# A rotary-embedding kernel: four neighbouring rows per partition, a cut first tile, and tables on another queue

## The chip, the cores and the metric

The kernel runs on one core of one Trainium2 chip. The metric is the device time of one execution in microseconds, as the median of several runs. The profile's span of the same execution is 1.8 to 2.1 us shorter than that time, mostly 1.8.

## The reference

```python
batch, seq, dim = 16, 512, 1024            # fp32, 33.5 MB in and 33.5 MB out
x = x.reshape(batch, seq, 16, 64)
x1, x2 = x[..., :32], x[..., 32:]
cos, sin = cos[None, :, None, :], sin[None, :, None, :]      # each (512, 32)
out = concatenate([x1 * cos - x2 * sin, x1 * sin + x2 * cos], axis=-1)
```

There is very little arithmetic for each byte. Every byte of x must come in once and every byte of the output must go out once.

## The kernel before

A tile is 128 sequence rows of four batches, 2 MB. Each partition holds one sequence row of each of the four batches, so what it holds lies in DRAM in four pieces of 4 KB, 2 MB apart. SyncE issues the loads. ScalarE converts a tile to bf16 and issues the stores. VectorE does two multiplies by tables that are stretched over heads, and then a subtraction and an addition that write fp32. There are three input buffers, two bf16 buffers and three output buffers. The last two tiles are cut into two and four pieces, and each piece takes a buffer of its own.

```python
if len(tiles) >= 2:
    t_last = tiles.pop()
    t_prev = tiles.pop()
    tiles += _split(t_prev, 2) + _split(t_last, 4)
...
NX = 3; NC = 2; NO = 3; NTMP = 2
...
cos_v = cos.rearrange("(sc p) j -> p sc j", p=P)              # pieces of 128 B
def x_tile_ap(t):
    sc, b0, nb = tiles[t]
    return x[b0:b0 + nb, sc * P:sc * P + P, :].rearrange("b s d -> s b d")   # pieces of 4 KB
...
# SyncE
for t in range(NT):
    if t >= NX:
        sp.wait_ge(sem_ci, t - NX + 1)          # the buffer's last tile has been converted
    sp.dma_start(x_sb[:, xb, 0:nb, :], x_tile_ap(t)).then_inc(sem_in[xb], 16)
    if t == 0:
        sp.dma_start(cos_sb[:], cos_v).then_inc(sem_tab, 16)
        sp.dma_start(sin_sb[:], sin_v).then_inc(sem_tab, 16)
...
# VectorE
ve.tensor_tensor(t1, xb_rows(cb, nb), coscat_b(sc, nb), mult)
ve.tensor_tensor(t2, xb_rows(cb, nb), sincat_b(sc, nb), mult).then_inc(sem_vp, 1)
if t >= NO:
    ve.wait_ge(sem_out[ob], 16 * (t // NO))     # the buffer's last store has landed
ve.tensor_tensor(orows[:, :, 0:HALF], t1[:, :, 0:HALF], t2[:, :, HALF:HD], subtract)
ve.tensor_tensor(orows[:, :, HALF:HD], t2[:, :, 0:HALF], t1[:, :, HALF:HD], add).then_inc(sem_vf, 1)
```

Of the kernel before, what the change touches and what calls it, by code (L numbers as in the profile page):

```python
# [7 lines left out]
def bass_split_heads_rope_kernel(  # L8
    nc: bass.Bass,
    x: bass.AP,  # L10
    cos: bass.AP,
    sin: bass.AP,
    num_heads: bass.AP,
    out: bass.AP,
):
    batch, seq, dim = x.shape
    H = int(num_heads)
    HD = dim // H
    HALF = HD // 2
    P = 128  # L20
    assert seq % P == 0
    NSC = seq // P

    NB = 4 if batch % 4 == 0 else batch
    tiles = []
    for sc in range(NSC):
        for b0 in range(0, batch, NB):
            tiles.append((sc, b0, NB))

    def _split(tile, parts):  # L30
        sc, b0, nb = tile
        if nb % parts != 0:
            return [tile]
        q = nb // parts
        return [(sc, b0 + i * q, q) for i in range(parts)]

    if len(tiles) >= 2:
        t_last = tiles.pop()
        t_prev = tiles.pop()
        tiles += _split(t_prev, 2) + _split(t_last, 4)  # L40
    NT = len(tiles)
    NBH = NB * H

    NX = 3
    NC = 2
    NO = 3
    NTMP = 2

    fp32 = mybir.dt.float32
    bf16 = mybir.dt.bfloat16  # L50
    mult = mybir.AluOpType.mult
    add = mybir.AluOpType.add
    subtract = mybir.AluOpType.subtract
    ACT_COPY = mybir.ActivationFunctionType.Copy

    with ExitStack() as stack:  # L56
        cos_sb = stack.enter_context(nc.sbuf_tensor([P, NSC, HALF], fp32))
        sin_sb = stack.enter_context(nc.sbuf_tensor([P, NSC, HALF], fp32))
        coscat_sb = stack.enter_context(nc.sbuf_tensor([P, NSC, HD], bf16))
        sincat_sb = stack.enter_context(nc.sbuf_tensor([P, NSC, HD], bf16))  # L60
        x_sb = stack.enter_context(nc.sbuf_tensor([P, NX, NB, dim], fp32))
        xb_sb = stack.enter_context(nc.sbuf_tensor([P, NC, NB, dim], bf16))
        o_sb = stack.enter_context(nc.sbuf_tensor([P, NO, NB, dim], fp32))
        tmp1_sb = stack.enter_context(nc.sbuf_tensor([P, NTMP, NBH, HD], bf16))
        tmp2_sb = stack.enter_context(nc.sbuf_tensor([P, NTMP, NBH, HD], bf16))
        sem_tab = stack.enter_context(nc.semaphore("sem_tab"))
        sem_tab2 = stack.enter_context(nc.semaphore("sem_tab2"))
        sem_in = [stack.enter_context(nc.semaphore(f"sem_in{i}")) for i in range(NX)]
        sem_out = [stack.enter_context(nc.semaphore(f"sem_out{i}")) for i in range(NO)]
        sem_ci = stack.enter_context(nc.semaphore("sem_ci"))  # L70
        sem_vp = stack.enter_context(nc.semaphore("sem_vp"))
        sem_vf = stack.enter_context(nc.semaphore("sem_vf"))
        block = stack.enter_context(nc.Block(no_gpsimd_drain=False))

        cos_v = cos.rearrange("(sc p) j -> p sc j", p=P)
        sin_v = sin.rearrange("(sc p) j -> p sc j", p=P)

        def x_tile_ap(t):
            sc, b0, nb = tiles[t]
            s0 = sc * P  # L80
            return x[b0:b0 + nb, s0:s0 + P, :].rearrange("b s d -> s b d")

        def out_tile_ap(t):
            sc, b0, nb = tiles[t]
            s0 = sc * P
            return out[b0:b0 + nb, s0:s0 + P, :, :].rearrange("b s h d -> s b (h d)")

        def xb_rows(cb, nb):
            return xb_sb[:, cb, 0:nb, :].rearrange("p b (h d) -> p (b h) d", h=H)

        def o_rows(ob, nb):
            return o_sb[:, ob, 0:nb, :].rearrange("p b (h d) -> p (b h) d", h=H)

        def coscat_b(sc, nb):
            return coscat_sb[:, sc, None, :].broadcast_to([P, nb * H, HD])

        def sincat_b(sc, nb):
            return sincat_sb[:, sc, None, :].broadcast_to([P, nb * H, HD])

        def uses(nbuf, b):  # L100
            return (NT - b + nbuf - 1) // nbuf

        @block.sync
        def _(sp):
            for t in range(NT):
                xb = t % NX
                _, _, nb = tiles[t]
                if t >= NX:
                    sp.wait_ge(sem_ci, t - NX + 1)
                sp.dma_start(x_sb[:, xb, 0:nb, :], x_tile_ap(t)).then_inc(sem_in[xb], 16)  # L110
                if t == 0:
                    sp.dma_start(cos_sb[:], cos_v).then_inc(sem_tab, 16)  # L112
                    sp.dma_start(sin_sb[:], sin_v).then_inc(sem_tab, 16)

        @block.scalar
        def _(ae):
            ae.wait_ge(sem_tab, 32)
            last = None
            for sc in range(NSC):
                last = ae.activation(coscat_sb[:, sc, 0:HALF], cos_sb[:, sc, :], ACT_COPY)  # L120
                last = ae.activation(coscat_sb[:, sc, HALF:HD], cos_sb[:, sc, :], ACT_COPY)  # L121
                last = ae.activation(sincat_sb[:, sc, 0:HALF], sin_sb[:, sc, :], ACT_COPY)  # L122
                last = ae.activation(sincat_sb[:, sc, HALF:HD], sin_sb[:, sc, :], ACT_COPY)  # L123
            assert last is not None
            last.then_inc(sem_tab2, 1)

            LEAD = 2
            for it in range(NT + LEAD):
                t = it
                if t < NT:  # L130
                    xb = t % NX
                    cb = t % NC
                    _, _, nb = tiles[t]
                    ae.wait_ge(sem_in[xb], 16 * (t // NX + 1))
                    if t >= NC:
                        ae.wait_ge(sem_vp, t - NC + 1)
                    ae.activation(  # L137
                        xb_sb[:, cb, 0:nb, :], x_sb[:, xb, 0:nb, :], ACT_COPY
                    ).then_inc(sem_ci, 1)
                u = it - LEAD  # L140
                if u >= 0:
                    ob = u % NO
                    _, _, nbu = tiles[u]
                    ae.wait_ge(sem_vf, u + 1)
                    ae.dma_start(out_tile_ap(u), o_sb[:, ob, 0:nbu, :]).then_inc(sem_out[ob], 16)
            for b in range(NO):
                ae.wait_ge(sem_out[b], 16 * uses(NO, b))

        @block.vector
        def _(ve):  # L150
            for t in range(NT):
                sc, _, nb = tiles[t]
                cb = t % NC
                tb = t % NTMP
                ob = t % NO
                nbh = nb * H
                if t == 0:
                    ve.wait_ge(sem_tab2, 1)
                ve.wait_ge(sem_ci, t + 1)
                if t >= NTMP:  # L160
                    ve.wait_ge(sem_vf, t - NTMP + 1)
                t1 = tmp1_sb[:, tb, 0:nbh, :]
                t2 = tmp2_sb[:, tb, 0:nbh, :]
                ve.tensor_tensor(t1, xb_rows(cb, nb), coscat_b(sc, nb), mult)  # L164
                ve.tensor_tensor(  # L165
                    t2, xb_rows(cb, nb), sincat_b(sc, nb), mult
                ).then_inc(sem_vp, 1)
                ve.wait_ge(sem_vp, t + 1)
                if t >= NO:
                    ve.wait_ge(sem_out[ob], 16 * (t // NO))  # L170
                orows = o_rows(ob, nb)
                ve.tensor_tensor(  # L172
                    orows[:, :, 0:HALF], t1[:, :, 0:HALF], t2[:, :, HALF:HD], subtract
                )
                ve.tensor_tensor(  # L175
                    orows[:, :, HALF:HD], t2[:, :, 0:HALF], t1[:, :, HALF:HD], add
                ).then_inc(sem_vf, 1)


# [31 lines left out]
```

## Time and profile before

| | before |
|---|---|
| time, median of 16 runs | 167.83 us |
| span of the profiled run (its own time: 168.56 us) | 166.7 us |
| bytes moved | 67.26 MB |
| DMA rate from 30 to 155 us | 421 GB/s |
| VectorE busy | 143.9 us |
| VectorE's first and last instruction | 14.37 and 163.6 us |

The profiled run was the slowest of these 16. The other runs of this kernel whose spans are listed have 165.9 to 166.3 us.

The page of the kernel before, in part: the row of DMA busy tenths over 40 equal slices of the span, the rate in each slice, and the packet count.

```profile
DMA  5999999999999999999999999999999999999974
GB/s 187 368 399 419 410 412 388 423 424 422 423 420 421 424 422 423 419 422 423 423 422 420 421 423 424 421 419 420 422 425 420 420 421 423 424 419 421 421 302 190
DMA packets 18082, 67.26 MB, mean 403 GB/s; under 512 B 1696, under 2 KB 1696, under 8 KB 18080
```

The DMA engines are busy from the first slice to the last. The packet count is the number of descriptors, and their sizes are those of the contiguous pieces: 16,384 records of 4 KB carry data and 1,024 of 128 B carry the tables. Nearly all of the rest, 672, have 4 B, which is 16 for each of the 42 DMAs; I take them for the semaphore updates.

The stretch table of the kernel before. A row gives a stretch of time, its length, the busy time of VectorE (DVE), ScalarE (ACT) and GpSimd (POOL) with their instruction counts, TensorE's clock, the DMA share and GB/s.

```profile
2.00:14.00 12.00, 0.00 (x0) 5.28 (x18) 0.00 (x0) 1.00 1.02 379
14.00:30.00 16.00, 15.56 (x7) 9.60 (x4) 0.00 (x0) 1.00 1.02 408
30.00:120.00 90.00, 88.75 (x41) 34.06 (x10) 0.00 (x0) 1.00 1.02 421
120.00:155.00 35.00, 31.12 (x21) 10.61 (x6) 0.00 (x0) 1.00 1.03 421
155.00:160.20 5.20, 5.13 (x9) 1.06 (x1) 0.00 (x0) 1.00 1.03 421
160.20:166.70 6.50, 3.37 (x6) 0.00 (x0) 0.00 (x0) 1.00 0.49 199
```

There are two losses around a steady 421 GB/s: a slow start, and 6.5 us at the end at 199 GB/s. In the middle both the DMA and VectorE are nearly full, so busy shares alone do not say which of them is the bound.

The timeline of the kernel before at three places: the tables arrive (8.74), VectorE starts (14.37), and in the tail the store of the last full tile is issued (141.87), VectorE waits (154.71) and finishes. Columns are start, duration, engine, line, operation, shapes, and the idle time before it with what ended it.

```profile
8.74 0.23 ACT L120 ACTIVATE coscat_sb<-cos_sb 128x32 bf16<-128x32 f32 x1 [6.72 <-DMA sin_sb<-in_sin_dram]
...
14.37 2.29 DVE L164 TENSOR_TENSOR tmp_sb<-xb_sb,coscat_sb 128x4096 bf16<-128x4096 bf16 x1 [14.37 <-ACT xb_sb L137]
...
141.87 0.38 ACTq L145 DMA_DIRECT2D out_dram<-o_sb  x1
...
154.71 0.69 DVE L172 TENSOR_TENSOR o_sb<-tmp_sb 128x512 f32<-128x512 bf16 x1 [2.34 <-DMA out_dram<-o_sb]
...
162.92 0.69 DVE L175 TENSOR_TENSOR o_sb<-tmp_sb 128x512 f32<-128x512 bf16 x1
```

The wait of 2.34 us at 154.71 is a quarter tile that waits for an output buffer. That buffer still holds the last full tile: its 2 MB store was issued at 141.87 and landed 12.75 us later, at 154.62. Only two half tiles of work lay between the two uses of the buffer.

### The profile page before, as it was taken

The numbers are of one execution on the slowest core, as the hardware profiler recorded it, in microseconds if no ns is written. First come the engines' busy times: TensorE is split into PE (matmuls) and PEld (weight loads), VectorE is DVE, ScalarE is ACT, GpSimd is POOL, SyncE is SP. The second block draws the span as 40 slices with busy tenths as digits, with TensorE's granted clock in tenths as the row PEclk, the third lists the DMA queues.
The fourth block names the chain that finished last, engine by engine and source line by source line (L and its number), as shares of the span: only waits on it lengthen the run. The fifth ranks groups of instructions, "written<-read, shape, count | busy, mean of one in ns | idle before, by whom it ended". The sixth has DMA issues, their size and how long they took to land.

```text
span 166.7 us, 242 instructions
## 1 busy us (share of the span) xinstructions
DVE 143.9 (86%) x80; ACT 61.9 (37%) x37; POOL 0.2 (0%) x4
## 2 busy tenths in 40 slices
DVE  0005999999999999999999999999798989995892
ACT  3099653517080807152441707135075012222200
POOL 0000000000000000000000000000000000000000
DMA  5999999999999999999999999999999999999974
GB/s 187 368 399 419 410 412 388 423 424 422 423 420 421 424 422 423 419 422 423 423 422 420 421 423 424 421 419 420 422 425 420 420 421 423 424 419 421 421 302 190
DMA packets 18082, 67.26 MB, mean 403 GB/s; under 512 B 1696, under 2 KB 1696, under 8 KB 18080
## 3 DMA queue, kind: packets, MB, share of 16 engines
q1 hardware_dynamic: 9568, 33.69, 50.2%
q10 hardware_dynamic: 8512, 33.56, 49.0%
q14 instruction: 2, 0.02, 0.0%
HBM read 33.69 MB, written 33.55 MB: 403 GB/s over the span
## 4 chain that ended last, share of the span: by engine, by line
DMA 51%; DVE 29%; issue 10%; ACT 6%; SPq 1%; DVEq 0%; ACTq 0%
DMA out_dram<-o_sb 32%; DMA x_sb<-in_x_dram 16%; DVE o_sb L175 10%; DVE tmp_sb L165 9%; DVE tmp_sb L164 8%; ACT xb_sb L137 5%; DMA sin_sb<-in_sin_dram 4%; DVE o_sb L172 2%; DVEq L56 0%; ACT coscat_sb L120 0%; SPq L112 0%; ACT sincat_sb L123 0%; ACT coscat_sb L121 0%; ACT sincat_sb L122 0%; SPq L110 0%
## 5 line engine op out<-in xcount | busy, mean ns | idle before, releaser
L137 ACT ACTIVATE xb_sb<-x_sb 128x4096 bf16<-128x4096 f32 (+2 forms) x20 | 58.7, 2933 | 89.0 <-DVE tmp_sb L165 61.7
L164 DVE TENSOR_TENSOR tmp_sb<-xb_sb,coscat_sb 128x4096 bf16<-128x4096 bf16 (+2 forms) x20 | 37.2, 1858 | 14.4 <-ACT xb_sb L137 14.4
L172 DVE TENSOR_TENSOR o_sb<-tmp_sb 128x2048 f32<-128x2048 bf16 (+2 forms) x20 | 37.3, 1865 | 5.3 <-DMA out_dram<-o_sb 4.8
L175 DVE TENSOR_TENSOR o_sb<-tmp_sb 128x2048 f32<-128x2048 bf16 (+2 forms) x20 | 37.2, 1859 | 0.0
L165 DVE TENSOR_TENSOR tmp_sb<-xb_sb,sincat_sb 128x4096 bf16<-128x4096 bf16 (+2 forms) x20 | 37.2, 1859 | 0.0
L120 ACT ACTIVATE coscat_sb<-cos_sb 128x32 bf16<-128x32 f32 x4 | 0.9, 217 | 6.7 <-DMA sin_sb<-in_sin_dram 6.7
L120 ACT ACT_TABLE_LOAD x1 | 1.3, 1283 | 0.7 <-PEq L193 0.7
L121 ACT ACTIVATE coscat_sb<-cos_sb 128x32 bf16<-128x32 f32 x4 | 0.9, 213 | 0.0
L123 ACT ACTIVATE sincat_sb<-sin_sb 128x32 bf16<-128x32 f32 x4 | 0.9, 213 | 0.0
L122 ACT ACTIVATE sincat_sb<-sin_sb 128x32 bf16<-128x32 f32 x4 | 0.9, 213 | 0.0
L193 POOL MEMSET const-bfloat16-1.0<- 128x1 bf16 x1 | 0.1, 102 | 0.0
L193 POOL MEMSET const-uint8-127<- 128x1 uint8 x1 | 0.1, 102 | 0.0
L193 POOL MEMSET const-float32-0.0<- 128x1 f32 x1 | 0.1, 99 | 0.2 <-issue 0.2
L193 POOL MEMSET const-float32-1.0<- 128x1 f32 x1 | 0.1, 99 | 0.0
## 6 DMA issues: line engine op xcount, KB each, us to landing
x_sb<-in_x_dram SPq DMA_DIRECT2D x14, 2048.0 KB, 20.3
out_dram<-o_sb ACTq DMA_DIRECT2D x14, 2048.0 KB, 18.9
x_sb<-in_x_dram SPq DMA_DIRECT2D x2, 1024.0 KB, 19.5
x_sb<-in_x_dram SPq DMA_DIRECT2D x4, 512.0 KB, 7.3
out_dram<-o_sb ACTq DMA_DIRECT2D x2, 1024.0 KB, 9.5
out_dram<-o_sb ACTq DMA_DIRECT2D x4, 512.0 KB, 3.1
cos_sb<-in_cos_dram SPq DMA_DIRECT2D x1, 64.0 KB, 7.1
sin_sb<-in_sin_dram SPq DMA_DIRECT2D x1, 64.0 KB, 7.0
```

Source lines behind the costliest of these rows:

```text
L120: last = ae.activation(coscat_sb[:, sc, 0:HALF], cos_sb[:, sc, :], ACT_COPY)
L121: last = ae.activation(coscat_sb[:, sc, HALF:HD], cos_sb[:, sc, :], ACT_COPY)
L122: last = ae.activation(sincat_sb[:, sc, 0:HALF], sin_sb[:, sc, :], ACT_COPY)
L123: last = ae.activation(sincat_sb[:, sc, HALF:HD], sin_sb[:, sc, :], ACT_COPY)
L137: ae.activation(xb_sb[:, cb, 0:nb, :], x_sb[:, xb, 0:nb, :], ACT_COPY).then_inc(sem_ci, 1)
L164: ve.tensor_tensor(t1, xb_rows(cb, nb), coscat_b(sc, nb), mult)
L165: ve.tensor_tensor(t2, xb_rows(cb, nb), sincat_b(sc, nb), mult).then_inc(sem_vp, 1)
L172: ve.tensor_tensor(orows[:, :, 0:HALF], t1[:, :, 0:HALF], t2[:, :, HALF:HD], subtract)
L175: ve.tensor_tensor(orows[:, :, HALF:HD], t2[:, :, 0:HALF], t1[:, :, HALF:HD], add).then_inc(sem_vf, 1)
L193: nc = _bacc.Bacc("TRN2", target_bir_lowering=False, num_devices=1)
```

## The change

The intent is longer contiguous runs in DRAM, an earlier start of VectorE, and a tail in small pieces. A tile is now one whole batch. Partition p holds sequence rows 4p to 4p+3, which are 16 KB in one run on both sides. The tables follow the same mapping (512 B per partition), move on ScalarE's queue beside the first load, and are stretched by four instructions instead of sixteen. The first tile is cut into two halves. The last is cut into a half and two quarters inside one buffer. The elementwise work is the same.

```diff
-    NB = 4 if batch % 4 == 0 else batch
-    ... tiles of (sc, b0, NB); last two split in 2 and 4 ...
+    SPP = seq // P          # 4 rows per partition
+    NT = batch
 ...
-            return x[b0:b0 + nb, s0:s0 + P, :].rearrange("b s d -> s b d")
+            return x[t, :, :].rearrange("(p j) d -> p (j d)", p=P)
 ... (the output and the tables alike)
+        HEAD = [2, 2]   # sequence rows per partition, first tile
+        TAIL = [2, 1, 1]   # the same, last tile
 ...
-                if t == 0:
-                    sp.dma_start(cos_sb[:], cos_v).then_inc(sem_tab, 16)
-                    sp.dma_start(sin_sb[:], sin_v).then_inc(sem_tab, 16)
+                if t == 0:
+                    for i, (j0, n) in enumerate(cuts(0)):
+                        sp.dma_start(x_sb[:, xb, j0 * dim:(j0 + n) * dim],
+                                     x_tile_ap(t)[:, j0 * dim:(j0 + n) * dim]).then_inc(sem_h[i], 16)
+                else:
+                    sp.dma_start(x_sb[:, xb, :], x_tile_ap(t)).then_inc(sem_in[xb], 16)
         def _(ae):
+            ae.dma_start(cos_sb[:].rearrange("p j d -> p (j d)"), cos_v.rearrange("p j d -> p (j d)")).then_inc(sem_tab, 16)
+            ae.dma_start(sin_sb[:].rearrange("p j d -> p (j d)"), sin_v.rearrange("p j d -> p (j d)")).then_inc(sem_tab, 16)
 ... (stores of the last tile, and VectorE's work of the first and last tile, piece by piece)
```

More of the change, by code (lines that the diff above doesn't have):

```diff
@@ L21, in bass_split_heads_rope_kernel @@
     assert seq % P == 0
-    NSC = seq // P
-    NB = 4 if batch % 4 == 0 else batch
-    tiles = []
-    for sc in range(NSC):
-        for b0 in range(0, batch, NB):
-            tiles.append((sc, b0, NB))
-    def _split(tile, parts):
-        sc, b0, nb = tile
-        if nb % parts != 0:
-            return [tile]
-        q = nb // parts
-        return [(sc, b0 + i * q, q) for i in range(parts)]
-    if len(tiles) >= 2:
-        t_last = tiles.pop()
-        t_prev = tiles.pop()
-        tiles += _split(t_prev, 2) + _split(t_last, 4)
-    NT = len(tiles)
-    NBH = NB * H
+    SPP = seq // P
+    ROWS = SPP * H
+    RE = ROWS * HD
+    NT = batch
     NX = 3
@@ L56, in bass_split_heads_rope_kernel @@
     with ExitStack() as stack:
-        cos_sb = stack.enter_context(nc.sbuf_tensor([P, NSC, HALF], fp32))
-        sin_sb = stack.enter_context(nc.sbuf_tensor([P, NSC, HALF], fp32))
-        coscat_sb = stack.enter_context(nc.sbuf_tensor([P, NSC, HD], bf16))
-        sincat_sb = stack.enter_context(nc.sbuf_tensor([P, NSC, HD], bf16))
-        x_sb = stack.enter_context(nc.sbuf_tensor([P, NX, NB, dim], fp32))
-        xb_sb = stack.enter_context(nc.sbuf_tensor([P, NC, NB, dim], bf16))
-        o_sb = stack.enter_context(nc.sbuf_tensor([P, NO, NB, dim], fp32))
-        tmp1_sb = stack.enter_context(nc.sbuf_tensor([P, NTMP, NBH, HD], bf16))
-        tmp2_sb = stack.enter_context(nc.sbuf_tensor([P, NTMP, NBH, HD], bf16))
+        cos_sb = stack.enter_context(nc.sbuf_tensor([P, SPP, HALF], fp32))
+        sin_sb = stack.enter_context(nc.sbuf_tensor([P, SPP, HALF], fp32))
+        coscat_sb = stack.enter_context(nc.sbuf_tensor([P, SPP, HD], bf16))
+        sincat_sb = stack.enter_context(nc.sbuf_tensor([P, SPP, HD], bf16))
+        x_sb = stack.enter_context(nc.sbuf_tensor([P, NX, RE], fp32))
+        xb_sb = stack.enter_context(nc.sbuf_tensor([P, NC, RE], bf16))
+        o_sb = stack.enter_context(nc.sbuf_tensor([P, NO, RE], fp32))
+        tmp1_sb = stack.enter_context(nc.sbuf_tensor([P, NTMP, ROWS, HD], bf16))
+        tmp2_sb = stack.enter_context(nc.sbuf_tensor([P, NTMP, ROWS, HD], bf16))
         sem_tab = stack.enter_context(nc.semaphore("sem_tab"))
@@ L69, in bass_split_heads_rope_kernel @@
         sem_out = [stack.enter_context(nc.semaphore(f"sem_out{i}")) for i in range(NO)]
+        sem_h = [stack.enter_context(nc.semaphore(f"sem_h{i}")) for i in range(2)]
         sem_ci = stack.enter_context(nc.semaphore("sem_ci"))
@@ L73, in bass_split_heads_rope_kernel, with xb_jhd, o_rows, cuts @@
         block = stack.enter_context(nc.Block(no_gpsimd_drain=False))
-        cos_v = cos.rearrange("(sc p) j -> p sc j", p=P)
-        sin_v = sin.rearrange("(sc p) j -> p sc j", p=P)
+        cos_v = cos.rearrange("(p j) d -> p j d", p=P)
+        sin_v = sin.rearrange("(p j) d -> p j d", p=P)
         def x_tile_ap(t):
-            sc, b0, nb = tiles[t]
-            s0 = sc * P
-            return x[b0:b0 + nb, s0:s0 + P, :].rearrange("b s d -> s b d")
+            return x[t, :, :].rearrange("(p j) d -> p (j d)", p=P)
         def out_tile_ap(t):
-            sc, b0, nb = tiles[t]
-            s0 = sc * P
-            return out[b0:b0 + nb, s0:s0 + P, :, :].rearrange("b s h d -> s b (h d)")
-        def xb_rows(cb, nb):
-            return xb_sb[:, cb, 0:nb, :].rearrange("p b (h d) -> p (b h) d", h=H)
-        def o_rows(ob, nb):
-            return o_sb[:, ob, 0:nb, :].rearrange("p b (h d) -> p (b h) d", h=H)
-        def coscat_b(sc, nb):
-            return coscat_sb[:, sc, None, :].broadcast_to([P, nb * H, HD])
-        def sincat_b(sc, nb):
-            return sincat_sb[:, sc, None, :].broadcast_to([P, nb * H, HD])
+            return out[t, :, :, :].rearrange("(p j) h d -> p (j h d)", p=P)
+        def xb_jhd(cb):
+            return xb_sb[:, cb, :].rearrange("p (j h d) -> p j h d", j=SPP, h=H)
+        def o_rows(ob):
+            return o_sb[:, ob, :].rearrange("p (r d) -> p r d", d=HD)
+        coscat_b = coscat_sb[:, :, None, :].broadcast_to([P, SPP, H, HD])
+        sincat_b = sincat_sb[:, :, None, :].broadcast_to([P, SPP, H, HD])
         def uses(nbuf, b):
             return (NT - b + nbuf - 1) // nbuf
+        HEAD = [2, 2]
+        TAIL = [2, 1, 1]
+        def cuts(t):
+            ns = HEAD if t == 0 else TAIL if t == NT - 1 else [SPP]
+            j0, res = 0, []
+            for n in ns:
+                res.append((j0, n))
+                j0 += n
+            assert j0 == SPP
+            return res
+        def before_(t):
+            return sum(len(cuts(u)) for u in range(t))
+        def casts_(t):
+            return len(HEAD) + t
         @block.sync
@@ L106, in _ @@
                 xb = t % NX
-                _, _, nb = tiles[t]
                 if t >= NX:
-                    sp.wait_ge(sem_ci, t - NX + 1)
-                sp.dma_start(x_sb[:, xb, 0:nb, :], x_tile_ap(t)).then_inc(sem_in[xb], 16)
+                    sp.wait_ge(sem_ci, casts_(t - NX))
                 if t == 0:
-                    sp.dma_start(cos_sb[:], cos_v).then_inc(sem_tab, 16)
-                    sp.dma_start(sin_sb[:], sin_v).then_inc(sem_tab, 16)
+                    for i, (j0, n) in enumerate(cuts(0)):
+                        sp.dma_start(
+                            x_sb[:, xb, j0 * dim:(j0 + n) * dim],
+                            x_tile_ap(t)[:, j0 * dim:(j0 + n) * dim],
+                        ).then_inc(sem_h[i], 16)
+                else:
+                    sp.dma_start(x_sb[:, xb, :], x_tile_ap(t)).then_inc(sem_in[xb], 16)
@@ L115, in _ @@
         @block.scalar
         def _(ae):
+            ae.dma_start(cos_sb[:].rearrange("p j d -> p (j d)"), cos_v.rearrange("p j d -> p (j d)")).then_inc(sem_tab, 16)
+            ae.dma_start(sin_sb[:].rearrange("p j d -> p (j d)"), sin_v.rearrange("p j d -> p (j d)")).then_inc(sem_tab, 16)
             ae.wait_ge(sem_tab, 32)
-            last = None
-            for sc in range(NSC):
-                last = ae.activation(coscat_sb[:, sc, 0:HALF], cos_sb[:, sc, :], ACT_COPY)
-                last = ae.activation(coscat_sb[:, sc, HALF:HD], cos_sb[:, sc, :], ACT_COPY)
-                last = ae.activation(sincat_sb[:, sc, 0:HALF], sin_sb[:, sc, :], ACT_COPY)
-                last = ae.activation(sincat_sb[:, sc, HALF:HD], sin_sb[:, sc, :], ACT_COPY)
@@ L124, in _, with store @@
-            assert last is not None
-            last.then_inc(sem_tab2, 1)
+            last = ae.activation(coscat_sb[:, :, 0:HALF], cos_sb[:, :, :], ACT_COPY)
+            last = ae.activation(coscat_sb[:, :, HALF:HD], cos_sb[:, :, :], ACT_COPY)
+            last = ae.activation(sincat_sb[:, :, 0:HALF], sin_sb[:, :, :], ACT_COPY)
+            last = ae.activation(sincat_sb[:, :, HALF:HD], sin_sb[:, :, :], ACT_COPY)
+            last.then_inc(sem_tab2, 1)
+            def store(u):
+                ob = u % NO
+                for i, (j0, n) in enumerate(cuts(u) if u == NT - 1 else [(0, SPP)]):
+                    done = before_(u) + i + 1 if u == NT - 1 else before_(u + 1)
+                    ae.wait_ge(sem_vf, done)
+                    ae.dma_start(
+                        out_tile_ap(u)[:, j0 * dim:(j0 + n) * dim],
+                        o_sb[:, ob, j0 * dim:(j0 + n) * dim],
+                    ).then_inc(sem_out[ob], 16)
@@ L132, in _ @@
                     cb = t % NC
-                    _, _, nb = tiles[t]
-                    ae.wait_ge(sem_in[xb], 16 * (t // NX + 1))
                     if t >= NC:
-                        ae.wait_ge(sem_vp, t - NC + 1)
-                    ae.activation(
-                        xb_sb[:, cb, 0:nb, :], x_sb[:, xb, 0:nb, :], ACT_COPY
-                    ).then_inc(sem_ci, 1)
-                u = it - LEAD
-                if u >= 0:
-                    ob = u % NO
-                    _, _, nbu = tiles[u]
-                    ae.wait_ge(sem_vf, u + 1)
-                    ae.dma_start(out_tile_ap(u), o_sb[:, ob, 0:nbu, :]).then_inc(sem_out[ob], 16)
+                        ae.wait_ge(sem_vp, before_(t - NC + 1))
+                    if t == 0:
+                        for i, (j0, n) in enumerate(cuts(0)):
+                            ae.wait_ge(sem_h[i], 16)
+                            ae.activation(
+                                xb_sb[:, cb, j0 * dim:(j0 + n) * dim],
+                                x_sb[:, xb, j0 * dim:(j0 + n) * dim], ACT_COPY
+                            ).then_inc(sem_ci, 1)
+                    else:
+                        ae.wait_ge(sem_in[xb], 16 * (t // NX + (0 if xb == 0 else 1)))
+                        ae.activation(xb_sb[:, cb, :], x_sb[:, xb, :], ACT_COPY).then_inc(sem_ci, 1)
+                if it - LEAD >= 0:
+                    store(it - LEAD)
             for b in range(NO):
-                ae.wait_ge(sem_out[b], 16 * uses(NO, b))
+                extra = len(TAIL) - 1 if b == (NT - 1) % NO else 0
+                ae.wait_ge(sem_out[b], 16 * (uses(NO, b) + extra))
         @block.vector
@@ L151, in _ @@
             for t in range(NT):
-                sc, _, nb = tiles[t]
                 cb = t % NC
@@ L155, in _ @@
                 ob = t % NO
-                nbh = nb * H
                 if t == 0:
                     ve.wait_ge(sem_tab2, 1)
-                ve.wait_ge(sem_ci, t + 1)
                 if t >= NTMP:
-                    ve.wait_ge(sem_vf, t - NTMP + 1)
-                t1 = tmp1_sb[:, tb, 0:nbh, :]
-                t2 = tmp2_sb[:, tb, 0:nbh, :]
-                ve.tensor_tensor(t1, xb_rows(cb, nb), coscat_b(sc, nb), mult)
-                ve.tensor_tensor(
-                    t2, xb_rows(cb, nb), sincat_b(sc, nb), mult
-                ).then_inc(sem_vp, 1)
@@ L168, in _ @@
-                ve.wait_ge(sem_vp, t + 1)
-                if t >= NO:
-                    ve.wait_ge(sem_out[ob], 16 * (t // NO))
-                orows = o_rows(ob, nb)
-                ve.tensor_tensor(
-                    orows[:, :, 0:HALF], t1[:, :, 0:HALF], t2[:, :, HALF:HD], subtract
-                )
-                ve.tensor_tensor(
-                    orows[:, :, HALF:HD], t2[:, :, 0:HALF], t1[:, :, HALF:HD], add
-                ).then_inc(sem_vf, 1)
+                    ve.wait_ge(sem_vf, before_(t - NTMP + 1))
@@ new lines, in _ @@
+                for i, (j0, n) in enumerate(cuts(t)):
+                    ve.wait_ge(sem_ci, i + 1 if t == 0 else casts_(t))
+                    r0, r1 = j0 * H, (j0 + n) * H
+                    t1 = tmp1_sb[:, tb, r0:r1, :]
+                    t2 = tmp2_sb[:, tb, r0:r1, :]
+                    t1v = t1.rearrange("p (j h) d -> p j h d", j=n)
+                    t2v = t2.rearrange("p (j h) d -> p j h d", j=n)
+                    ccat = coscat_sb[:, j0:j0 + n, None, :].broadcast_to([P, n, H, HD])
+                    scat = sincat_sb[:, j0:j0 + n, None, :].broadcast_to([P, n, H, HD])
+                    xin = xb_jhd(cb)[:, j0:j0 + n]
+                    ve.tensor_tensor(t1v, xin, ccat, mult)
+                    ve.tensor_tensor(t2v, xin, scat, mult).then_inc(sem_vp, 1)
+                    ve.wait_ge(sem_vp, before_(t) + i + 1)
+                    if t >= NO and i == 0:
+                        ve.wait_ge(sem_out[ob], 16 * (t // NO))
+                    orows = o_rows(ob)[:, r0:r1]
+                    ve.tensor_tensor(
+                        orows[:, :, 0:HALF], t1[:, :, 0:HALF], t2[:, :, HALF:HD], subtract
+                    )
+                    ve.tensor_tensor(
+                        orows[:, :, HALF:HD], t2[:, :, 0:HALF], t1[:, :, HALF:HD], add
+                    ).then_inc(sem_vf, 1)
```

## The prediction

> **What bounds the kernel now.** The DMA engines. The stretch table shows 420 to 422 GB/s from 30 to 158 us. 67.26 MB at 421 GB/s are 159.8 us of the 166.7 us span. VectorE looks just as full (143.9 us busy, from 14.37 to 163.6), but its 16 tiles cost 8.93 us each against 9.96 us of DMA for a tile in and out (4.19 MB at 421). It keeps up because the loads ran up to five tiles ahead while it started late.
>
> **Where 6.9 us of the span are not full-rate DMA** (stretch table): about 1.9 us before the first bytes; about 1.2 us between 2 and 14 us, where the rate is 330 to 406 and 1,024 table descriptors of 128 B are being moved; 0.5 us from 14 to 30 us; and about 3.4 us after 160 us, where the rate falls to 184 to 248 while VectorE finishes.
>
> **What the change does.**
> 1. Each partition holds four neighbouring sequence rows, so a full-tile descriptor becomes 16 KB instead of 4 KB, on both sides. The page counts 18,082 packets (16,384 of data); I expect about 5,300. [...] No run here shows 16 KB yet[...].
> 2. Tables: 256 descriptors of 512 B on the other queue. About 1 us of the early loss goes.
> 3. Head: half tile, tables in parallel, four table copies instead of sixteen. VectorE starts at about 7.5 us instead of 14.37. Not worth 7 us: the DMA, the bound, has queued loads all that time. It gives VectorE slack at the end.
> 4. Tail: with that slack VectorE ends about 5 us before the DMA, and the last tile's pieces share one output buffer instead of using up three. The last stores then run at full rate; about 2 us of the 3.4 go, the last store's latency stays.
> 5. VectorE: same elements, inner runs of 64; a full-tile multiply stays at 2285 ns, the total at 143 to 144 us.
>
> **Sum.** 166.7 - 2.3 - 1.0 - 2.0 = 161.4 us of span. The median time before is 1.3 us above the profiled span, so 162.8 us, range 160.8 to 165.3. Chances: faster by over 2% (under 164.6) 0.80, within 2% 0.19, slower 0.01.
>
> **What would show each step.** (1) the packet count, and a steady rate of 427 or more in the middle stretches; (2) the second and third slices at 400 or more; (3) VectorE's first multiply at 7 to 8.5 us; (4) no DMA slice but the last below 400, VectorE's last instruction several us before the end, the end of the chain of waits made of DMA; VectorE waits over the 4.8 us of before; (5) the multiply's duration.
>
> **What would make it wrong.** Rate unchanged at 421: about 165, on the edge of "same". Loads and stores of 16 KB sharing the engines less evenly, so that VectorE starves: then the tail is long (about 16 us from last load to end). [...]

A note on step 1 and the sum. The 2.3 us and the 427 GB/s that stand in the sum and among the signs were the author's estimate, without a measurement behind it. With the term the sum came to 161.4 us of span and 162.8 us of time; without it, it would be 163.7 and 165.0.

## The result

| | before | after |
|---|---|---|
| time, median | 167.83 us (16 runs) | 162.75 us (8 runs) |
| ratio | | 0.9687, 95% interval 0.9675 to 0.9699 |
| span of the profiled run | 166.7 us | 160.9 us |
| DMA rate, 30 to 120 us | 421 GB/s | 431 GB/s |
| VectorE's first and last instruction | 14.37 and 163.6 us | 11.79 and 156.3 us |

A ratio is the mean time of one kernel's runs over that of the other's in the same rounds, so it is not quite the ratio of the medians quoted beside it. The same lines of the changed kernel's page:

```profile
DMA  5999999999999999999999999999999999999996
GB/s 158 432 445 420 440 416 391 407 444 436 412 456 407 440 444 403 456 420 428 452 407 444 436 411 456 401 444 444 407 452 420 428 456 395 452 432 416 456 393 263
DMA packets 5330, 67.25 MB, mean 418 GB/s; under 512 B 593, under 2 KB 849, under 8 KB 1105
```

The slices now jump by tens of GB/s. I read that as an effect of longer records in short slices (in the trace's records of single descriptors, which no view prints, one of 16 KB takes 611 ns, by the median, of a slice of 4.0 us, and one of 4 KB before took 159 ns), and use longer stretches. Its stretch table:

```profile
2.00:14.00 12.00, 2.21 (x2) 5.77 (x8) 0.00 (x0) 1.00 1.01 409
14.00:30.00 16.00, 15.90 (x11) 10.51 (x3) 0.00 (x0) 1.00 1.01 417
30.00:120.00 90.00, 89.65 (x42) 32.71 (x10) 0.00 (x0) 1.00 1.01 431
120.00:155.00 35.00, 34.50 (x22) 10.70 (x3) 0.00 (x0) 1.00 1.00 427
155.00:158.00 3.00, 1.30 (x3) 0.00 (x0) 0.00 (x0) 1.00 1.00 419
158.00:160.90 2.90, 0.00 (x0) 0.00 (x0) 0.00 (x0) 1.00 0.49 199
```

The two tables make a ledger of the 5.8 us of span, worked out at 421 GB/s:

- Up to 30 us the changed kernel has moved about 550 KB more, which is 1.3 us.
- From 30 to 155 us it moves 10 GB/s more for 90 us and 6 GB/s more for 35 us. That is 1.1 MB, or 2.6 us.
- After 155 us the kernel before needs 11.7 us for what would take 8.3 at 421, and the changed one 5.9 us for what would take 4.4. The gain is 1.9 us.

Of these 5.8 us about 0.7 belong to the profiled run of before, which was slower than its usual runs. The trace does not say in which part.

The timeline of the changed kernel, where the tables arrive, where VectorE starts and where it ends:

```profile
8.97 0.31 ACT L121 ACTIVATE coscat_sb<-cos_sb 128x128 bf16<-128x128 f32 x1 [6.04 <-DMA sin_sb<-in_sin_dram]
...
11.79 1.23 DVE L181 TENSOR_TENSOR tmp_sb<-xb_sb,coscat_sb 128x2048 bf16<-128x2048 bf16 x1 [11.79 <-ACT xb_sb L148]
...
155.65 0.68 DVE L190 TENSOR_TENSOR o_sb<-tmp_sb 128x512 f32<-128x512 bf16 x1
```

The tables come no earlier than before (8.97 against 8.74). VectorE starts earlier because the table copies take 0.8 us instead of 1.9, and because it needs the cast of half a tile (1.9 us) instead of a whole one (3.6 us).

The waits of the changed kernel (total us, how often, longest):

```profile
ACT xb_sb L154 <- DMA x_sb<-in_x_dram: 49.1, 9, 6.3
...
DVE o_sb L187 <- DMA out_dram<-o_sb: 0.4, 1, 0.4
```

Casts waited 27.3 us for loads before the change and wait 49.1 us now, but VectorE waits only 0.4 us once it has started. So VectorE's own chain is nearly gapless: its start at 11.79, 144.5 us to its end (143.6 of them busy), then one last store. Two chains, the DMA's and VectorE's, end within about 2 us of each other. The prediction had treated VectorE as having room to spare, and the experiments test that.

### The profile page after: what moved, and what is told of

The parts are those of the page before. It is cut to its first block, busy times and chain, and to the rows that moved or that the text cites. A ratio compares the mean times of both kernels' runs of the same rounds, so it can differ in the third digit from the quotient of the medians.

```text
span 160.9 us, 206 instructions
## 1 busy us (share of the span) xinstructions
DVE 143.6 (89%) x76; ACT 60.0 (37%) x22; POOL 0.2 (0%) x4
## 2 busy tenths in 40 slices
DMA packets 5330, 67.25 MB, mean 418 GB/s; under 512 B 593, under 2 KB 849, under 8 KB 1105
## 3 DMA queue, kind: packets, MB, share of 16 engines
q10 hardware_dynamic: 2880, 33.69, 49.1%
## 4 chain that ended last, share of the span: by engine, by line
DMA 60%; DVE 26%; ACT 6%; issue 4%; DVEq 0%; ACTq 0%
DMA x_sb<-in_x_dram 31%; DMA out_dram<-o_sb 23%; DVE o_sb L190 8%; DVE tmp_sb L181 7%; DVE tmp_sb L182 7%; DMA sin_sb<-in_sin_dram 5%; ACT xb_sb L154 5%; DVE o_sb L187 4%; ACT xb_sb L148 1%; DVEq L40 0%; ACTq L118 0%; ACT coscat_sb L121 0%; ACT sincat_sb L124 0%; ACT sincat_sb L123 0%; ACT coscat_sb L122 0%
## 5 line engine op out<-in xcount | busy, mean ns | idle before, releaser
L154 ACT ACTIVATE xb_sb<-x_sb 128x4096 bf16<-128x4096 f32 x15 | 54.3, 3617 | 75.1 <-DMA x_sb<-in_x_dram 49.1
L181 DVE TENSOR_TENSOR tmp_sb<-xb_sb,coscat_sb 128x4096 bf16<-128x4096 bf16 (+2 forms) x19 | 37.0, 1947 | 11.8 <-ACT xb_sb L148 11.8
L148 ACT ACTIVATE xb_sb<-x_sb 128x2048 bf16<-128x2048 f32 x2 | 3.7, 1892 | 0.0
L121 ACT ACTIVATE coscat_sb<-cos_sb 128x128 bf16<-128x128 f32 x1 | 0.3, 309 | 6.0 <-DMA sin_sb<-in_sin_dram 6.0
L123 ACT ACTIVATE sincat_sb<-sin_sb 128x128 bf16<-128x128 f32 x1 | 0.3, 293 | 0.0
L124 ACT ACTIVATE sincat_sb<-sin_sb 128x128 bf16<-128x128 f32 x1 | 0.3, 293 | 0.0
L122 ACT ACTIVATE coscat_sb<-cos_sb 128x128 bf16<-128x128 f32 x1 | 0.3, 292 | 0.0
```

The lines of the kernel that those rows point to most:

```text
L121: last = ae.activation(coscat_sb[:, :, 0:HALF], cos_sb[:, :, :], ACT_COPY)
L122: last = ae.activation(coscat_sb[:, :, HALF:HD], cos_sb[:, :, :], ACT_COPY)
L123: last = ae.activation(sincat_sb[:, :, 0:HALF], sin_sb[:, :, :], ACT_COPY)
L124: last = ae.activation(sincat_sb[:, :, HALF:HD], sin_sb[:, :, :], ACT_COPY)
L148: ae.activation(xb_sb[:, cb, j0 * dim:(j0 + n) * dim], x_sb[:, xb, j0 * dim:(j0 + n) * dim], ACT_COPY).then_inc(sem_ci, 1)
L154: ae.activation(xb_sb[:, cb, :], x_sb[:, xb, :], ACT_COPY).then_inc(sem_ci, 1)
```

## The experiments

The theories are these. **A**: the DMA is the bound, the gain is fewer descriptors plus a better tail, and VectorE's start is only slack. **B**: the steady rate rose because DRAM is walked in another order. **C**: VectorE's chain is the bound, and the gain is its earlier start. All outputs were correct. "Changed" means the kernel after the change, 162.75 us. The kernel before, run beside them, had medians of 167.78 to 168.0 us.

| run | median us | ratio to before | GB/s, 30 to 120 us | VectorE starts |
|---|---|---|---|---|
| changed | 162.75 | 0.9687 | 431 | 11.79 |
| 8 KB descriptors | 163.98 | 0.9771 | 427 | 11.9 |
| 4 KB, even and odd rows | 170.81 | 1.0173 | 414 | 12.0 |
| 4 KB, padded rows | 165.96 | 0.9887 | 421 | 10.79 |
| 2 KB | 171.07 | 1.0190 | 409 | 11.9 |
| first tile whole | 167.47 | 0.9975 | | 18.33 |
| last tile whole | 164.33 | 0.9791 | | 11.8 |
| tables in 128 B | 171.95 | 1.0243 | | 21.53 |
| tables first | 163.82 | 0.9749 | | 8.95 |
| tables second | 163.27 | 0.9729 | | 9.18 |
| new mapping, old start | 163.53 | 0.9730 | 431 | 13.46 |
| before, with a new tail | 166.08 | 0.9895 | 421 | 14.35 |
| before, tables first | 168.46 | 1.0038 | | 13.27 |

### Descriptor size: 8, 4 and 2 KB

The runs with two DMAs per tile share this edit. `cut` gives the two contiguous halves (8 KB), or the even and the odd pieces (4 and 2 KB).

```diff
-                    sp.dma_start(x_sb[:, xb, :], x_tile_ap(t)).then_inc(sem_in[xb], 16)
+                    for d, s in zip(cut(x_sb[:, xb, :]), cut(x_tile_ap(t))):
+                        sp.dma_start(d, s).then_inc(sem_in[xb], 16)
 ... (stores alike; waits on these semaphores count 32 per tile)
+        def cut(ap):      # 8 KB
+            return [ap[:, 0:2 * dim], ap[:, 2 * dim:4 * dim]]
+        def cut(ap):      # 4 KB; for 2 KB e=512
+            return [ap.rearrange("p (a b e) -> p a b e", b=2, e=1024)[:, :, i] for i in range(2)]
```

> The changed kernel, but every full tile moves as two DMAs of 1 MB, one per contiguous half of each partition's 16 KB, so descriptors of 8 KB. Theory A (a fixed cost per descriptor, worked out from the steady-rate gain of 2.6 us for 16,384 minus about 4,500 data descriptors, so about 3.5 ns on each of 16 engines): about 0.8 us slower than the changed kernel's 162.75 us, so 163.5, and a steady rate near 429. Theory B (the gain came from the order in which DRAM is walked): no change, 162.7 within 0.4. It is also the control for the cost of two DMAs per tile.

> The changed kernel, but every full tile moves as two DMAs of 1 MB, the even and the odd sequence rows of each partition, so descriptors of 4 KB as before the change; the DRAM region of a tile, the tile order, head, tail and tables are those of the changed kernel. Theory A: 2.5 us slower than the changed kernel, about 165.3 us, with a steady rate back at 421. Theory B: within 0.4 us of 162.75 and of the 8 KB run.

> As the 4 KB run with two interleaved DMAs per tile, but descriptors of 2 KB (about 30,700 of data). Theory A, linear in the number of descriptors: about 6 us slower than the changed kernel, 168.5 to 169, steady rate about 412. Theory B: within 0.4 us of 162.75.

Measured: 163.98, 170.81 and 171.07 us. The 8 KB run came 0.5 us above what A expected of it. The 2 KB run came 2 us above; the cost per descriptor turned out larger than I had put in (below). The 4 KB run did not fit at all: it is as slow as 2 KB. It changes the walk of DRAM too (all even rows of a tile, then all odd rows), so it could not tell A from B. A cleaner 4 KB run was needed. Padding each row in SBUF cuts the descriptors and leaves one DMA per tile and the walk as they are:

```diff
-        x_sb = stack.enter_context(nc.sbuf_tensor([P, NX, RE], fp32))
+        x_sb = stack.enter_context(nc.sbuf_tensor([P, NX, SPP, dim + 16], fp32))
 ... (o_sb alike; accesses take [..., 0:dim])
```

> The changed kernel, but each sequence row has 64 B of padding behind it in SBUF, on the x and the output side, so that every DMA moves 4 KB descriptors with DRAM walked as in the changed kernel and one DMA per tile. The runs with 2 and 8 KB and the two kernels fit a fixed cost of about 4.8 ns per descriptor; on that theory this run loses 768 more descriptors per engine, 3.7 us: 166.4 us, steady rate 421. If it comes out at 170 to 171 as the run with even and odd rows did (rate 411 to 414 until 90 us), 4 KB is slow in this layout by itself; if near 166.4, that run lost its other 4 us to the interleaved walk of DRAM. The tables should land earlier than 8.95, near 5 to 6 us[...].

Measured: 165.96 us, 0.4 us below the forecast, at the forecast rate of 421. The tables landed at 7.97 us and not at 5 to 6, which is a miss (the next section returns to it). The stretch tables of the two 4 KB runs, first the one with even and odd rows:

```profile
2.00:14.00 12.00, 1.96 (x2) 5.44 (x7) 0.00 (x0) 1.00 0.96 363
14.00:30.00 16.00, 15.90 (x11) 10.85 (x3) 0.00 (x0) 1.00 1.02 402
30.00:120.00 90.00, 85.84 (x40) 30.96 (x9) 0.00 (x0) 1.00 1.02 414
```

And the one with padded rows:

```profile
2.00:14.00 12.00, 3.18 (x3) 5.55 (x8) 0.00 (x0) 1.00 0.99 393
14.00:30.00 16.00, 15.93 (x11) 10.82 (x3) 0.00 (x0) 1.00 1.02 414
30.00:120.00 90.00, 88.42 (x41) 32.56 (x9) 0.00 (x0) 1.00 1.02 421
```

The same stretch of the runs with 2 KB and with 8 KB:

```profile
30.00:120.00 90.00, 85.66 (x40) 32.32 (x9) 0.00 (x0) 1.00 1.05 409
...
30.00:120.00 90.00, 89.65 (x42) 32.55 (x9) 0.00 (x0) 1.00 1.01 427
```

With the changed kernel's walk and 4 KB descriptors the steady rate is exactly that of the kernel before, 421 GB/s. So the steady gain of the change is the descriptor size, and B falls as its explanation. The time of one descriptor on one of 16 engines follows from the rate: 16 x 2,048 B / 409 GB/s is 80.1 ns, and in the same way 155.7 ns for 4 KB (421), 306.6 for 8 KB (427.3) and 608.6 for 16 KB (430.7; the last two rates are means of three stretches of 30 us). From 4 to 8 KB that is 151.0 ns more, from 8 to 16 KB 302.0, from 2 to 4 KB 75.6. The line is straight, and it leaves about 4.7 ns per descriptor at each size from 2 to 16 KB. This is an estimate from the measured rates; they are rounded, so it is good to about half a nanosecond. Going from 1,024 data descriptors per engine to 280 (256 of 16 KB, were all tiles whole) is then worth 744 x 4.7 ns = 3.5 us. Measured between the padded run and the changed kernel: 3.2 us.

The walk may matter in its own way. The interleaved 4 KB run lost 4.9 us against the padded one, at 414 GB/s with the engines just as busy. It also has two DMAs per tile, but the 8 KB run has those too and lost only 1.2 us in all. The loss is not steady, though. The rate is 411 GB/s from 30 to 60 us, 414 to 90 us, 417 to 120 us and 420 from 120 to 155 us, against 421 in the padded run throughout; and the last 2.4 us of the span run at 48 GB/s. In the trace's records of single descriptors (no view prints them) the median is 159 ns in both runs, and the slow run has some that take longer (mean 161.7 against 159.1 ns, 30 to 120 us). So this is not a fixed price of the walk. Why it is slow at first, while 2 KB pieces 4 KB apart lie on the line, stays open.

### The head: first tile whole, and where the tables queue

```diff
-        HEAD = [2, 2]
+        HEAD = [4]
```

> The changed kernel with its first tile loaded, cast and computed whole. Theory A (the DMA is the bound, and VectorE's early start is only slack): VectorE starts 1.5 to 2.5 us later, the time rises by 0 to 0.9 us. Rival C (VectorE's chain from its start to its end is the bound): the time rises by as much as the start, 1.5 to 2.5 us.

Measured: 167.47 us, 4.7 us more than changed. Both theories missed the size, because VectorE started 6.5 us later and not 2. The timeline shows why:

```profile
13.81 0.31 ACT L121 ACTIVATE coscat_sb<-cos_sb 128x128 bf16<-128x128 f32 x1 [10.89 <-DMA sin_sb<-in_sin_dram]
...
18.33 2.29 DVE L181 TENSOR_TENSOR tmp_sb<-xb_sb,coscat_sb 128x4096 bf16<-128x4096 bf16 x1 [18.33 <-ACT xb_sb L148]
```

The 64 KB tables landed 4.8 us later, though their own transfers are unchanged. What changed is the load beside them: its descriptors are now 16 KB instead of 8. In the changed kernel's records of single descriptors the two queues start about equally many: in each us from 4 to 7, 48 of the tables' (512 B) and 48 or 49 of the load's (8 KB). A rule is not shown by this: beside the 4 KB descriptors of the padded run the tables landed at 7.97 us, only 1.0 earlier than beside 8 KB. The next edit leaves the loads alone and makes the table descriptors four times as many:

```diff
-        cos_sb = stack.enter_context(nc.sbuf_tensor([P, SPP, HALF], fp32))
+        cos_sb = stack.enter_context(nc.sbuf_tensor([P, SPP, HALF + 32], fp32))
 ... (sin_sb alike)
-            ae.dma_start(cos_sb[:].rearrange("p j d -> p (j d)"), cos_v.rearrange("p j d -> p (j d)"))
+            ae.dma_start(cos_sb[:, :, 0:HALF], cos_v)
```

> The changed kernel with table rows padded in SBUF so that the tables move as 1,024 descriptors of 128 B instead of 256 of 512 B, still on ScalarE's queue. Theory A (small table descriptors cost DMA time at the start): 0.3 to 0.8 us slower than 162.75, the last table lands 1 to 4 us later than 8.95, VectorE starts later by as much. Rival (table descriptors cost no DMA time): within 0.2 us.

Measured: 171.95 us, 9.2 us more than changed. I had expected at most 0.8. The first table copy, and the stretches around it:

```profile
18.72 0.31 ACT L121 ACTIVATE coscat_sb<-cos_sb 128x128 bf16<-128x128 f32 x1 [15.36 <-DMA sin_sb<-in_sin_dram]
```

```profile
14.00:16.00 2.00, 0.00 (x0) 0.00 (x0) 0.00 (x0) 1.00 0.97 413
16.00:18.00 2.00, 0.00 (x0) 0.00 (x0) 0.00 (x0) 1.00 0.80 311
18.00:20.00 2.00, 0.00 (x0) 1.28 (x5) 0.00 (x0) 1.00 0.01 2
20.00:22.00 2.00, 0.47 (x1) 2.00 (x2) 0.00 (x0) 1.00 0.00 0
22.00:24.00 2.00, 1.97 (x3) 2.00 (x2) 0.00 (x0) 1.00 0.00 0
```

The DMA stands idle from about 18 to past 24 us. The chain is this. ScalarE's program has the tables first, then the casts, and the timeline shows them in that order (first table copy at 18.72, first cast at 19.53). The tables land at 18.7, so no cast has run by then, no input buffer has been freed, and all three loads (6.3 MB, which take 14.6 us at 431 GB/s) are done by about 17. The fourth load must wait. In the run with the first tile whole the same thing happens in a small way: the first cast ends at 18.2, and the DMA drops to 131 GB/s between 18 and 20 us.

Two bounds then account for the run with the first tile whole. VectorE starts at 18.33, works 143.2 us, stands still for 1.0 us (0.4 of it for buffers) and ends at 162.5; the span ends 3.1 us later, with the last store, at 165.6. That is C's arithmetic. The run with 128 B tables fits it too: VectorE ends at 166.9, and the span 3.1 us later, at 170.0. In the changed kernel the same sum is 11.79 + 144.5 = 156.3 plus 3.1, or about 159.4, while the span is 160.9: 4.6 us pass after VectorE's end, because other stores were still ahead of the last one (the last half tile's moved until 157.6, by its descriptor records). So VectorE has about 1.5 us of slack in the changed kernel. Within that slack A holds, beyond it C does.

Now the tables are put in front of everything, or between the two halves of the first tile, on SyncE's queue, so that no load stands beside them on another queue:

```diff
         def _(sp):
+            sp.dma_start(cos_sb..., cos_v...).then_inc(sem_tab, 16)
+            sp.dma_start(sin_sb..., sin_v...).then_inc(sem_tab, 16)
             for t in range(NT):
 ... ("tables second": the two lines stand behind the first half of the first tile instead)
         def _(ae):
-            ae.dma_start(cos_sb..., cos_v...).then_inc(sem_tab, 16)
-            ae.dma_start(sin_sb..., sin_v...).then_inc(sem_tab, 16)
```

> The changed kernel with both table loads issued on SyncE's queue ahead of the first tile, instead of on ScalarE's queue beside it. The tables should land by about 3 to 4 us instead of 8.95 and VectorE start at 7.5 to 9 us instead of 11.8, which is what the prediction had counted on. Theory A (DMA-bound): the time stays within 0.5 us of 162.75, and what VectorE gains at the start it loses in waits in the middle (over 2 us instead of 0.4). Rival C (VectorE's chain is the bound): 3 us faster, about 160.

> The changed kernel with the two table loads on SyncE's queue between the first and the second half of the first tile, instead of on ScalarE's queue. [...] they now land at 5 to 7 us and VectorE starts at 8 to 9.5 us. Theory A (DMA-bound): 162.3 to 162.9 us, no better than the changed kernel by more than 0.4. Rival C (VectorE's chain is the bound): 2.5 to 3 us faster.

Measured: 163.82 and 163.27 us. The tables landed at 3.1 and 6.4 us, and VectorE started at 8.95 and 9.18. Both are slightly slower than changed, by 1.1 and 0.5 us, against my expectation of at most half a microsecond either way for the first and no loss for the second. C, which wanted about 3 us less, is refuted. What VectorE gained at the start became waits: casts waited 80.7 us for loads in both runs, instead of 49.1. The loss arises at the start: by 30 us the first run had moved 0.49 MB less than changed and the second 0.37 MB less, which is 1.1 and 0.9 us at 431 GB/s. For the first run most of this is visible, as the first load is issued 0.9 us later. For the second I have no cause. Neither version beats the changed kernel.

The start of the kernel before, with the new mapping and the new tail:

```diff
-        HEAD = [2, 2]
+        HEAD = [4]
 ... (tables taken off ScalarE's queue; cos_sb and sin_sb padded, so 128 B descriptors)
                         ).then_inc(sem_h[i], 16)
+                    sp.dma_start(cos_sb[:, :, 0:HALF], cos_v).then_inc(sem_tab, 16)
+                    sp.dma_start(sin_sb[:, :, 0:HALF], sin_v).then_inc(sem_tab, 16)
```

> The changed kernel's 16 KB descriptors and its tail, but the start of the kernel before: the first tile whole, the tables as 128 B descriptors behind it on SyncE's queue. VectorE starts at 13 to 15 us. Theory A: the steady rate is that of the changed kernel (428 to 433), the time 0.8 to 2 us above 162.75, because a later VectorE ends after the DMA could. Rival C: later by the whole delay of VectorE's start, 2 to 3 us.

Measured: 163.53 us, 0.8 above changed, at the same steady rate of 431. This run differs from "first tile whole" only in the tables, which are cut finer and queue behind the first tile on SyncE. They land at 8.94 instead of 13.81, and the run is 3.9 us faster. Of the change's three early steps (the cut head, the wider table rows, the other queue) the other queue is the one that can do harm, and the cut head and the wide rows are what keep it harmless.

In the kernel before, the table loads alone were moved ahead of the first tile:

```diff
+                if t == 0:
+                    sp.dma_start(cos_sb[:], cos_v).then_inc(sem_tab, 16)
+                    sp.dma_start(sin_sb[:], sin_v).then_inc(sem_tab, 16)
                 sp.dma_start(x_sb[:, xb, 0:nb, :], x_tile_ap(t)).then_inc(sem_in[xb], 16)
-                if t == 0:
-                    ... the same two lines ...
```

> The kernel before with its two table loads (128 B descriptors) issued ahead of the first tile on the same queue. VectorE starts about 2 us earlier than 14.37. Theory A (the DMA is the bound, and an earlier start of VectorE is worth nothing): 167.3 to 168.5. Rival C (VectorE's chain is the bound): 1.5 to 2 us faster, about 166.

Measured: 168.46 against 167.78 us. VectorE started 1.1 us earlier (13.27) and nothing was gained. C is refuted for the kernel before as well. All three edits also put the tables ahead of x, or of a part of it, on SyncE's queue. So they show that an earlier start gained nothing on balance, and not what it would be worth alone.

### The tail

```diff
-        TAIL = [2, 1, 1]
+        TAIL = [4]
```

> The changed kernel with its last tile computed and stored whole. Theory A (the tail's gain is that the last store is small and issued while others still run): the last 2 MB store is issued when VectorE ends, near 155.5 us, and needs at least 5 us of movement and over 1 us of latency: the span ends near 162, the time rises by 1 to 1.5 us, and one or two of the last DMA slices drop. Rival (the tail does not matter, stores are queued anyway): within 0.3 us of 162.75.

Measured: 164.33 us, 1.6 us more than changed, just above what A expected. Its stretch table at the end:

```profile
150.00:155.00 5.00, 4.96 (x3) 0.00 (x0) 0.00 (x0) 1.00 0.86 370
155.00:160.00 5.00, 1.26 (x1) 0.00 (x0) 0.00 (x0) 1.00 0.62 262
```

The other stores run out before VectorE has finished the whole last tile at 156.3, and then 2 MB are still to go. The span ends at 163.0, 6.7 us later; 2 MB at 421 GB/s would be 5.0 of these. Last, the kernel before with a tail like the new one:

```diff
-        tiles += _split(t_prev, 2) + _split(t_last, 4)
+        sc, b0, _ = t_last
+        tiles += [t_prev, (sc, b0, 2), (sc, b0 + 2, 1), (sc, b0 + 3, 1)]
```

> The kernel before, with the last two tiles cut as 4, 2, 1, 1 batches instead of 2, 2, 1, 1, 1, 1. If the tail's 2 us of the prediction come from the small tiles that use up buffers: 0.5 to 2 us faster than 167.83. If they come from VectorE's earlier end (which this run does not have): within 0.5 us.

Measured: 166.08 us, 1.7 us faster than before, with VectorE starting no earlier than there (14.35). Its stretch table at the end:

```profile
155.00:160.00 5.00, 4.93 (x8) 0.00 (x0) 0.00 (x0) 1.00 1.02 421
160.00:164.30 4.30, 0.99 (x2) 0.00 (x0) 0.00 (x0) 1.00 0.65 265
```

The small tail of the kernel before was too small. VectorE ends at 161.0 us in this run instead of 163.6, though the expectation had supposed that it would not end earlier: its waits for output buffers fall from 4.8 to 2.9 us, and its busy time from 143.9 to 143.2. In the kernel before, one tile of work in two halves lay between the last full tile and the next use of its buffer, and VectorE waited 2.34 us for that tile's store; here it is a tile and a half, and that wait is gone. An edit of two lines in the kernel before is worth a third of the whole change.

## Why the prediction was right

The time and the sign were right: 162.8 predicted, 162.75 measured. The parts were less exact than that.

- **The bound.** It said the DMA. In both kernels moving VectorE's start earlier gained nothing on balance (168.46 against 167.78; 163.27 and 163.82 against 162.75), so this holds. That it "keeps up" with room was too loose: the whole-head run shows only about 1.5 us of slack in the changed kernel.
- **Step 1, descriptors: 2.3 us.** The effect is shown, the size was too small: 3.2 us measured between padded 4 KB and 16 KB, 3.5 from 4.7 ns per descriptor. Packets were predicted at about 5,300 and are 5,330; the rate was predicted at 427 and is 431. The 2.3 us were the author's estimate, made before any run of this case had another descriptor size; only the runs from 2 to 16 KB measure the cost. What the 4.7 ns consist of is not shown by any run here.
- **Step 2, tables: 1.0 us.** About right in the ledger, wrong in its cause. By 30 us the changed kernel is 1.3 us ahead, but about 0.6 of that is the higher rate (10 of 421 GB/s over 28 us), as worked out from the steady stretch. The many small table descriptors are not the rest: with them back on SyncE's queue (old start) the DMA had moved only 84 KB less by 30 us, or 0.2 us. The experiments put head and tables together at 0.8 us (old start, 163.53), in a run that VectorE's end bounds (158.4, and the span 3.1 us later). "On the other queue" was counted as a gain, and the runs with 16 KB neighbours and with 128 B table rows show that it is a risk of 4 to 9 us.
- **Step 3, VectorE's start: 7.5 us.** Wrong: 11.79. The tables landed at 8.97, because they shared the engines with large load descriptors (48 and 48 or 49 starts in each us from 4 to 7). In front of the loads they land by 3.1 us. It cost nothing, because, as the step also said, the start is not the bound; but a delay of more than about 1.5 us would have made it one.
- **Step 4, tail: 2.0 us.** Right: 1.9 in the ledger, 1.7 from the tail alone in the kernel before, 1.6 from undoing the cut in the changed kernel. The reason given first, VectorE's slack, is not needed for it, since the tail alone gains as much without an earlier start. The reason given second, the buffers, is supported by VectorE's shorter waits in that run, but not in the form given: its three last pieces still take a buffer each. What helped there was more work between two uses of a buffer.
- **Step 5, VectorE's work.** Right, as the groups by shape show (line, engine, operation, tiles, shapes, count, total us, mean ns, idle time). Before:

```profile
L165 DVE TENSOR_TENSOR tmp_sb<-xb_sb,sincat_sb 128x4096 bf16<-128x4096 bf16 x14 | 32.0, 2285 | 0.0
```

After:

```profile
L182 DVE TENSOR_TENSOR tmp_sb<-xb_sb,sincat_sb 128x4096 bf16<-128x4096 bf16 x14 | 32.0, 2285 | 0.0
```

- **The sum.** It came out closer than its terms. The span was predicted at 161.4 and was 160.9. The prediction then added 1.3 us to get the time, by setting the median of all runs against the span of one slow run; within one run the difference is about 1.8. Two errors of half a microsecond cancelled, and that is luck. The effects measured one at a time (3.2, 0.8 and 1.6 us) add up to 5.6 against 5.1 for the whole change, so they overlap a little.
- **The signs it named.** The second and third slices (432, 445) and VectorE's end 4.6 us before the end of the span came as told. VectorE's waits "over the 4.8 us" did not: it waits 0.4 us once started, and the waits sit with ScalarE's casts. Slices below 400 exist (391, 393, 395), and the page's chain is followed back from the last instruction, which is VectorE's in both kernels, so "made of DMA" was not a usable sign.

What stays open: why the rate from 14 to 30 us is low in every kernel looked at (417 against 431 in the changed one; its descriptor records have the 16 KB loads at 638 ns on average there, against 611 ns from 30 to 90 us, and the stores at 611 ns), why the interleaved 4 KB run loses 4.9 us, and why the tables in second place cost 0.5 us.

## What to carry to other kernels

In a kernel bound by DMA, count descriptors: here each cost about 4.7 ns of its engine (an estimate from the rates), the same from 2 to 16 KB, so the layout that gives a partition one run of 16 KB instead of four of 4 KB was worth 2.3% of the rate (421 to 430.7 GB/s). Watch a small transfer that gates the start and is queued beside large ones on another queue: here the 64 KB tables landed at 8.97 us beside 8 KB descriptors and at 13.81 beside 16 KB ones, against 3.1 in front of the loads. Look at when it lands, and at how long the loads can go on before the first buffer must come free. Do not cut the tail into so many tiles, each in a buffer of its own, that VectorE comes round to a buffer whose store is still on its way (2.34 us of waiting here). And before crediting "an earlier start", move the start alone and see whether the time follows.
